# Attention stage: buffers of the first three weight blocks, engine of the last query rotation, and places of the value stores, a broadcast and five transpositions

## The chip, the core and the metric

The kernel runs on one core of a Trainium2 chip. The core has a matrix engine (TensorE, PE; its weight loads are shown apart as PEld), a vector engine (VectorE, DVE), a scalar engine (ScalarE, ACT), a general engine (GpSimd, POOL) and a queue engine (SyncE, SP) that only issues transfers. Each engine works through its own instructions in order; transfers (DMA) are issued by SP, ACT and POOL and run on 16 shared DMA engines. The metric is the device time of one launch in microseconds (us); less is better.

## The reference

One inference step of a two-layer encoder for 512 new tokens and 64 tokens of a running stream, 576 in all, 1024 features wide, in float32. Layer 0 mixes tokens by causal pooling; layer 1 is attention. Each is followed by an MLP with squared ReLU, and every sub-layer has an RMS normalisation ahead of it:

```python
for i in range(DEPTH):
    h = _rmsnorm(x, norm_mix[i])
    y = pool_mixer(h) if i == 0 else attn_mixer(h)
    x = x + y
    x = x + (relu(_rmsnorm(x, norm_mlp[i]) @ w_up[i]) ** 2) @ w_down[i]
```

The attention projects `h` by one matrix into 16 query heads of 64, 4 key and 4 value heads, 8 indexer queries of 64, one indexer key of 64 and 8 indexer weights. Queries, keys, indexer queries and indexer key are rotated: `x1*c - x2*s, x2*c + x1*s`, with halves x1, x2 of each head. The indexer scores `sum_h relu(qi_h . ki) * wi_h` select the best keys of each token (256, or fewer when there are few); softmax attention goes over the selected keys alone. New keys, values and indexer keys are outputs too.

## The kernel before

**Layout.** Activations lie with features on the 128 partitions and tokens along the free dimension, eight tiles of 128 x 576. Every float32 matrix product is done as three reduced-precision ones: each operand is split into an upper part (`act.copy`, line 206 for weights, 316 for activations) and a remainder (`dve.tensor_tensor`, lines 207 and 317), and upper x upper, remainder x upper and upper x remainder are summed in PSUM.

**Weights.** Weights come as blocks of 128 x 1024 (512 KB). One generator, `loaded`, holds the order of all blocks of the kernel (`jobs`, each with a kind), starts their loads some blocks ahead, and `next_block` hands out the split block; two more are kept split ahead (`AHEAD = 2`). A load needs a landing buffer from `raw_tile` (lines 139 to 145): in the stages of pooling and MLP the pool `raws` has two buffers, and a second pool `more` has two more, which are open only to loads called with `mlp=True`; these take turns, turns 0 and 1 of four to `raws`, 2 and 3 to `more`. Loads with `mlp=True` are issued by SP, the others by ACT. The split block itself takes one of three buffers of `weights`. In the attention stage the memory of `more` belongs to the pool `under`, which holds a pad, the rotation tables `cs` and `sn` and two masks.

**MLP of layer 0.** Its downward products go in pairs of output tiles by a scheme with seven products in place of eight. A pair (class `Pair`) has the products b11 and b21 in bank a, t1 and b22 in bank c, and t2, t3 and t4 in a seeded bank ("seed" in the rows). Between t3 and t4 VectorE must take t3 out of the bank into x (line 490); after opening, lines 486 do the same with a minus sign. The last pair's t4 ends the MLP.

**Attention.** `attention` (line 1087 on) first scales and splits x into `xs` (lines 316, 317), sends x to DRAM for later (`xd`, line 1093), and loads `cs` and `sn`. With TensorE's order written out by hand (`manual_schedule`) come the two indexer projections of the first four heads (`project_qi`, "pi" in the rows, 24 matmuls of 448 columns each), the token sums of the norm, the broadcast of the norm's factor over the partitions (two "rb" matmuls, evicted by ACT, line 357) and the indexer key ("ki"). POOL and VectorE multiply the factor into `cs` and `sn` (lines 1121, 1122). Then the indexer queries are rotated by VectorE (`rope` with `started`), the key is rotated, the eight indexer weights are transposed by five small "pw" matmuls (line 1197) into `wi` (line 1198), the other four indexer heads are projected, and the key and four query groups follow (`rope_q`, "pj"). For those ACT copies the two projections out of PSUM (lines 1150, 1151), POOL does four products, a difference and a sum with 576 columns (lines 1152 to 1158), ACT and POOL split the result (1161, 1162), and eight transfers of SP put it into DRAM as `qd` (line 1182). Index scores and the ranking of the keys (`top_k`, line 1258 on) run on VectorE beside this. Last comes the value projection ("v", line 1460), evicted by ACT to `V` (line 1462), and two stores of it by SP (lines 1463, 1464).

The scores, softmax, transpositions and value products follow as 40 units; two units share a `Group`, whose queries SP loads from `qd` (line 1349) into one of three slots with the tag "a". The groups go key head by key head for the first two blocks of 128 tokens, then block by block.

**What sets the order.** Except where `manual_schedule` fixes it, a planner orders the instructions of every engine and queue by a simulated timeline; `tc.issue_after` adds constraints to it.

Of the kernel before, what the change touches and what calls it, by code (L numbers as in the profile page):

```python
# [12 lines left out]
ALU = mybir.AluOpType  # L13
# [3 lines left out]
P = 128  # L17
D = 1024
KT = D // P
TP = 512  # L20
TS = 64
T = TP + TS
HT = T // 2
NKV = 4
NIDX = 8
# [26 lines left out]
def pool_dsa_kernel(ctx: ExitStack, tc: tile.TileContext, a, o):  # L52
    nc = tc.nc
    act, dve, pool, pe = nc.scalar, nc.vector, nc.gpsimd, nc.tensor
# [51 lines left out]
    def psum1(s="po", pool="po"):  # L106
        return phase[pool].tile([P, 512], F32, tag="po", name=uid(s))
# [12 lines left out]
    ident = const([P, P], "ident")  # L120
# [16 lines left out]
    last_of = {}  # L137
# [16 lines left out]
    jobs = []  # L154
# [32 lines left out]
                jobs.append(("made", "down", c, q) if layer else ("pair", *rows("down", layer, c, q)))  # L187

    mlp_jobs(0, 4, PLAIN[0])
    jobs.extend(("w_ki" if j == 0 else "w_in", a["w_in"][j]) for j in (1, 2, 0, *range(3, 15)))  # L190
    jobs.extend(("w_v", a["w_v"][j]) for j in range(2))
    for kind in ("w_o", "w_o2"):
        jobs.extend((kind, a["w_o"][m]) for m in range(KT))
# [53 lines left out]
    def loaded():  # L247

        waiting, held = [], 0
        while jobs or waiting:  # L250
            while jobs and held < (4 if "more" in phase else 2 if "third" in phase else 1) and ("last" in phase or jobs[0][0] not in ("pair", "made")):
                kind, *srcs = jobs.pop(0)
                if kind == "made":
                    r1, r2 = rows(srcs[0], 1, *srcs[1:])
                    m = mixed[:, pairs[tuple(srcs)]].rearrange("p a b -> p (a b)")
                    srcs = [r1, m[:, 1024:], m[:, :1024], r2[:, 512:]]
                mlp = kind in ("mlp", "pair", "made", "w_o2")
                waiting.append((kind, [load(src, src.shape[1], nc.sync if mlp else act, mlp)[:, :src.shape[1]] for src in srcs]))
                held += len(srcs)
            kind, tiles = waiting.pop(0)  # L260
            held -= len(tiles)
            yield kind, tiles
# [53 lines left out]
            act.activation(dst[:, 0], src, AF.Copy, scale=scale)  # L316
            dve.scalar_tensor_tensor(dst[:, 1], src, scale, f32(dst[:, 0]), ALU.mult, ALU.subtract)

    def project(pt, w, xs, between=iter(()), cols=((0, HT), (HT, HT)), ks=range(KT), ends=None):

        for k in ks:
            next(between, None)
            wh, wl = at(w, k)
            for i, (wt, part) in enumerate(((wh, 0), (wh, 1), (wl, 0))):
                for h, (c, m) in enumerate(cols):
                    pe.matmul(  # L326
                        pt[h][:, :m] if isinstance(pt, tuple) else pt[:, h, :m], wt, xs[k][:, part, c:c + m],
                        start=(k == (ends or ks)[0] and i == 0), stop=(k == (ends or ks)[-1] and i == 2),
                    )

    class Norm:
# [755 lines left out]
    def attention(parts):  # L1087
        nonlocal x
        norm = Norm("a")
        xs = split_x(2, norm, ["xs"] * KT)  # L1090
# [4 lines left out]
        cs, sn = (const([P, T], s, pool=phase["under"]) for s in ("cs", "sn"))  # L1095
        nc.sync.dma_start(cs, a["cos"])
        nc.sync.dma_start(sn, a["sin"])
        V = const([P, 9, 256], "V", pool=phase["cst1"])
        wi = const([P, 5, 8], "wi", pool=cst)
        nc.sync.dma_start(V[:, 4:8], a["cache_v"])  # L1100


        def project_qi(amid=None):
            pt = psum1("pi")
            w = next_block()
            for ks in (range(KT - 2), range(KT - 2, KT)) if amid else (range(KT),):
                if ks[0]:
                    amid()
                project((pt,), w, xs, cols=((P, T - P),), ks=ks, ends=(0, KT - 1))
            return pt[:, :T - P]  # L1110

        with tc.manual_schedule(engines={ENG.PE}):
            q0 = [project_qi()]
            norm.stats()
            r = norm.r
            two = psum("rb")
            q0.append(project_qi(lambda: norm.spread((two[:, 0], two[:, 1]))))
            rb = norm.rb
            pki = psum("ki")
            project(pki, next_block(), xs)  # L1120
        pool.tensor_tensor(cs, cs, rb, ALU.mult)
# [7 lines left out]
            split(t[:, :, :TP], raw[:, :TP], None, sub)  # L1129
            return t  # L1130

        def rope(started=None):

            pts = started
            if not started:
                pts = []
                for _ in range(2):
                    pt = psum("pj")
                    project(pt, next_block(), xs, between)
                    pts.append(pt[:, :, :HT])  # L1140
            n = T - P if started else T
            a1, b2, b1, a2 = (tmp("rp", "rp", 4)[:, :n] for _ in range(4))
            if started:
                pa, pb = pts
                dve.tensor_tensor(a1, pa, cs[:, P:], ALU.mult)
                dve.tensor_tensor(a2, pa, sn[:, P:], ALU.mult)
                dve.tensor_tensor(b2, pb, sn[:, P:], ALU.mult)
                dve.tensor_tensor(b1, pb, cs[:, P:], ALU.mult)
            else:
                act.copy(halves(a1), pts[0])  # L1150
                act.copy(halves(b1), pts[1])
                pool.tensor_tensor(a2, a1, sn, ALU.mult)
                pool.tensor_tensor(a1, a1, cs, ALU.mult)
                pool.tensor_tensor(b2, b1, sn, ALU.mult)
                pool.tensor_tensor(b1, b1, cs, ALU.mult)
            eng = dve if started else pool
            eng.tensor_tensor(a1, a1, b2, ALU.subtract)
            eng.tensor_tensor(b1, b1, a2, ALU.add)
            st = [pair_slot("b", "st")[:, :, :n] for _ in range(2)]
            for j, t in enumerate((a1, b1)):  # L1160
                act.copy(st[j][:, 0], t)
                pool.tensor_tensor(st[j][:, 1], t, f32(st[j][:, 0]), ALU.subtract)
            return (a1, b1), st
# [3 lines left out]
        def rope_qi(g, started):  # L1167

            _, st = rope(started)
            for h in range(4):  # L1170
                for j in range(2):
                    for part in range(2):
                        at = part * 64 + j * 32
                        nc.sync.dma_start(f32(qi[at:at + 32, 4 * g + h]), f32(st[j][32 * h:32 * h + 32, part]))

        def rope_q(s):

            _, st = rope()
            qd = dram.tile([4, 2, 2, 32, T], F32, tag=s, name=s)
            for h in range(4):  # L1180
                for j in range(2):
                    nc.sync.dma_start(qd[h, :, j].rearrange("a p t -> p a t"), f32(st[j][32 * h:32 * h + 32]))
            return qd.rearrange("h a j p t -> (a j p) h t")

        between = iter(())
# [3 lines left out]
        wt = tmp("wt")  # L1189
        act.copy(halves(wt[0:32]), pki[0:32, :, :HT])  # L1190
        for to, first, table in ((t1, 96, cs), (t2, 64, sn)):
            for i, c in enumerate((first, 160 - first)):
                dve.tensor_tensor(halves(to[32 * i:32 * i + 32]), pki[c:c + 32, :, :HT], halves(table[c:c + 32]), ALU.mult)
        pw = psum1("pw")
        for i in range(5):
            n = P if i < 4 else TS
            pe.transpose(pw[:n, 32 * i:32 * i + 32], wt[0:32, i * P:i * P + n], ident[0:32, 0:32])
            dve.tensor_scalar(wi[:n, i], pw[:n, 32 * i:32 * i + NIDX], r[:n, i:i + 1], NIDX ** -0.5, ALU.mult, ALU.mult)
        dve.tensor_tensor(ki[0:32], t1[0:32], t2[0:32], ALU.subtract)
        dve.tensor_tensor(ki[32:64], t1[32:64], t2[32:64], ALU.add)  # L1200
        nc.sync.dma_start(o["ki"], ki[0:64])
# [5 lines left out]

        cki = split_cache(a["cache_ki"], "cki", kis)

        rope_qi(1, [project_qi() for _ in range(2)])  # L1210

        work = [None] + [const([P, (i + 1) * P if i < 4 else TP + TS], f"work{i}", pool=phase[("cst1", "under", "under", "cst2")[i - 1]]) for i in range(1, 5)]

# [186 lines left out]
        def steps():  # L1400

            ranked = {0}
            for u in range(-4, total + 2):
                if 0 <= u + 4 < total and units[u + 4].s == 0:
                    v = units[u + 4]
                    groups[v.i, v.g] = Group(v.i, v.g)
                if 0 <= u < total:
                    units[u].transpose()
                if 0 <= u + 2 < total:
                    v = units[u + 2]  # L1410
                    if u + 2 >= 8:
                        next(index, None)
                    if v.i not in ranked:
                        ranked.add(v.i)
                        while done[0] < v.i * NIDX and next(index, 1) is None:
                            pass
                        top_k(v.i)
                    v.scores()
                if 0 <= u - 1 < total:
                    units[u - 1].values()  # L1420
                if 0 <= u - 2 < total and units[u - 2].s == 1:
                    units[u - 2].group.outputs()
                if u >= 18 and u % 2 == 0:
                    next(first_out, None)
                yield

        def pace():
# [20 lines left out]
                nc.sync.dma_start(f32(t[32 * c:32 * c + 32]), f32(st[c % 2][32 * g:32 * g + 32]))  # L1448
            ks.append(t)
        for g in range(NKV):  # L1450
            qd[g] = rope_q(f"q{g}")
        wv = [next_block(), next_block()]
        for i in range(5):
            n = P if i < 4 else TS
# [5 lines left out]
                    pe.matmul(pt[:n, :256], xs[k][:, part, i * P:i * P + n], wt,  # L1460
                              start=(k == 0 and j == 0), stop=(k == KT - 1 and j == 2))
            act.activation(V[:n, i if i < 4 else 8], pt[:n, :256], AF.Copy, scale=r[:n, i:i + 1])
        nc.sync.dma_start(o["v_p"], V[:, 0:4])
        nc.sync.dma_start(o["v_s"], V[:TS, 8])
        parts.close()
        parts.enter_context(stage(ps=3, po=2))
        for _ in steps():
# [125 lines left out]
```

## Time and profile before

| what | value |
|---|---|
| median of 3 runs | 1115.61 us (1115.17 to 1118.61) |
| profiled execution, its own time | 1115.93 us |
| its span in the profile | 1114.2 us |
| mean granted TensorE clock | 0.989 |
| TensorE busy | 97% of the span |
| VectorE, ScalarE, GpSimd busy | 71%, 50%, 26% |

The first layer's MLP ends near 441 us of the span; attention lasts until about 722 us; the second MLP fills the rest. A row of a timeline gives the start, the time until the group's end, engine, line, operation, output and inputs, shapes, count, and in brackets the idle time before it with the instruction that ended it. A row of the waits gives who waited for whom, microseconds in total, times and the longest. In a matrix engine's row the instructions overlap, so a row can be longer than the time until the next one starts.

### The profile page before, as it was taken

What the parts mean: (1) busy time and instruction counts of PE and PEld (TensorE: products, weight loads), DVE (VectorE), ACT (ScalarE), POOL (GpSimd) and SP (SyncE); (2) the same over time, 40 slices, a digit from 0 to 9 for tenths busy, and PEclk for the clock granted to TensorE, in tenths of its full rate; (3) what the DMA queues carried; (4) which work ended last, traced back from release to release, by engine and by line L of the source; (5) the groups of instructions that cost most, each with busy time, mean ns of one, the idle gap of its engine ahead of it and who ended that gap; (6) DMA issues with size and microseconds to landing.
All of it is one profiled execution on the core that took longest, in us unless ns stands there. A gap on an engine that the chain in (4) does not pass through costs nothing.

```text
span 1114.2 us, 20339 instructions
## 1 busy us (share of the span) xinstructions
PE 1082.3 (97%) x8027; PEld 1064.7 (96%) x8027; DVE 791.3 (71%) x1441; ACT 556.4 (50%) x939; POOL 295.2 (26%) x227
## 2 busy tenths in 40 slices
PE   8999999999999998999989999999999999999995
PEld 8999999999999988899979999999999999999995
DVE  7767656665755787679679993778758867865644
ACT  7544334334433454444378665755536636644542
POOL 2005514531451642157935342001000000000002
PEclk9999999999999998999989999999999999999998
DMA  7266489479668979357642432448575655455402
GB/s 238 62 166 160 134 225 273 118 201 268 158 171 232 243 205 251 106 154 190 188 150 58 126 97 93 141 124 218 163 235 176 197 166 165 157 161 171 143 19 85
DMA packets 81263, 183.54 MB, mean 165 GB/s; under 512 B 11809, under 2 KB 23376, under 8 KB 81168
## 3 DMA queue, kind: packets, MB, share of 16 engines
q1 hardware_dynamic: 64512, 143.94, 39.2%
q0 software_dynamic: 13056, 25.17, 13.7%
q10 hardware_dynamic: 3600, 13.14, 3.7%
q8 instruction: 63, 1.03, 0.4%
q14 instruction: 32, 0.26, 0.1%
HBM read 167.14 MB, written 61.22 MB: 205 GB/s over the span
## 4 chain that ended last, share of the span: by engine, by line
PE 73%; DVE 7%; DMA 7%; POOL 5%; issue 4%; ACT 3%; SPq 0%; DVEq 0%; POOLq 0%; ACTq 0%
PE seed L429 14%; PE up L587 13%; PE c L429 9%; PE a L429 9%; PE pj L326 6%; PE dn L326 4%; PE o L1334 3%; DVE w L207 2%; DMA raw<-in_w_down 2%; PE wa L326 2%; PE pi L326 2%; DMA mixed<-mixed 2%; PE sc L1295 1%; PE z L949 1%; PE pt L1315 1%
## 5 line engine op out<-in xcount | busy, mean ns | idle before, releaser
L206 ACT CAST w<-raw 128x1024 fp32r<-128x1024 f32 (+2 forms) x242 | 211.0, 889 | 215.8 <-PE seed L429 82.6
L207 DVE TENSOR_TENSOR w<-raw,w 128x1024 fp32r<-128x1024 f32 (+2 forms) x224 | 246.7, 1108 | 61.9 <-ACT w L206 61.3
L587 PE MATMUL up<-xs,w 128*128 128x288 f32 x1536 | 206.3, 295 | 0.0
L587 PEld LDWEIGHTS up<-xs,w 128*128 128x128 f32 x1536 | 204.0, 188 | 0.2
L429 PE MATMUL seed<-u,w 128*128 128x288 f32 x1008 | 147.9, 298 | 6.3 <-DVE x L490 3.3
L429 PEld LDWEIGHTS seed<-u,w 128*128 128x128 f32 x1008 | 139.4, 190 | 7.9 <-DVE x L490 3.5
L429 PE MATMUL c<-u,w 128*128 128x288 f32 x672 | 100.9, 297 | 2.0 <-DVE w L207 1.2
L429 PE MATMUL a<-u,w 128*128 128x288 f32 x672 | 100.0, 295 | 1.5 <-ACT w L206 1.2
L429 PEld LDWEIGHTS c<-u,w 128*128 128x128 f32 x672 | 93.2, 188 | 3.2 <-DVE w L207 1.7
L429 PEld LDWEIGHTS a<-u,w 128*128 128x128 f32 x672 | 93.0, 188 | 2.3 <-ACT w L206 1.7
L812 POOL TENSOR_TENSOR x<-x,spare 128x320 f32<-128x320 f32 (+1 forms) x9 | 8.2, 943 | 232.9 <-ACT spare L808 232.9
L326 PE MATMUL pj<-xs,w 128*128 128x288 f32 x480 | 67.7, 295 | 0.0
L236 POOL DMA_DIRECT2D mixed<-in_w_up x24 | 28.0, 1210 | 144.5 <-DMA mixed<-mixed 100.3
L326 PEld LDWEIGHTS pj<-xs,w 128*128 128x128 f32 x480 | 65.4, 188 | 0.9
L236 POOL DMA_DIRECT2D mixed<-in_w_down x24 | 27.6, 1274 | 139.7 <-DMA mixed<-mixed 88.9
L429 PE MATMUL seed<-bx,w 128*128 128x288 f32 x432 | 62.5, 296 | 0.0
L207 DVE TENSOR_TENSOR w<-sum,w 128x1024 fp32r<-128x1024 f32 (+1 forms) x32 | 34.6, 1080 | 37.0 <-ACT w L206 36.9
L285 POOL TENSOR_TENSOR sum<-raw 128x512 f32<-128x512 f32 x16 | 26.4, 1647 | 127.2 <-DMA raw<-in_w_down 119.4
L429 PEld LDWEIGHTS seed<-bx,w 128*128 128x128 f32 x432 | 59.3, 188 | 0.1
L206 ACT CAST w<-sum 128x1024 fp32r<-128x1024 f32 (+1 forms) x32 | 26.7, 834 | 59.8 <-POOL sum L290 52.9
L722 DVE SCALAR_TENSOR_TENSOR v<-up,rbm 128x288 f32<-128x288 f32 x80 | 32.6, 450 | 31.9 <-PE up L587 29.0
L587 PE MATMUL up<-bx,w 128*128 128x288 f32 x288 | 51.0, 295 | 0.7 <-DVE x L1481 0.7
(298 smaller groups left out, 2027.6 us busy)
## 6 DMA issues: line engine op xcount, KB each, us to landing
raw<-in_w_up SPq DMA_DIRECT2D x52, 512.0 KB, 5.0
raw<-in_w_down SPq DMA_DIRECT2D x52, 512.0 KB, 4.3
raw<-mixed SPq DMA_DIRECT2D x48, 512.0 KB, 4.2
mixed<-in_w_down POOLq DMA_DIRECT2D x24, 512.0 KB, 7.9
mixed<-mixed SPq DMA_DIRECT2D x24, 512.0 KB, 7.9
mixed<-in_w_up POOLq DMA_DIRECT2D x24, 512.0 KB, 9.5
raw<-in_w_in ACTq DMA_DIRECT2D x15, 512.0 KB, 4.0
mixed<-in_w_down SPq DMA_DIRECT2D x12, 512.0 KB, 6.3
```

The costliest lines, as they stand in the source:

```text
L206: act.copy(w[:, 0, at], src[:, at])
L207: how["sub"].tensor_tensor(w[:, 1, at], src[:, at], f32(w[:, 0, at]), ALU.subtract)
L236: pool.dma_start(to, add, accum_op=ALU.add)
L285: pool.tensor_tensor(s[:, :512], r2[:, :512], r2[:, 512:], ALU.add)
L326: pe.matmul(pt[h][:, :m] if isinstance(pt, tuple) else pt[:, h, :m], wt, xs[k][:, part, c:c + m], start=(k == (ends or ks)[0] and i == 0), ...
L429: pe.matmul(bank[:, :HT], wt[:, at], ut, start=first and j == 0 and i == 0, stop=j == 3 and i == 2, skip_group_check=True)
L587: pe.matmul(pt[h][:, :HT], w[:, wt, k * P:(k + 1) * P], moving(k, part, h), start=n == 0 and i == 0, stop=n == KT - 1 and i == 2)
L722: dve.scalar_tensor_tensor(v[:, 2 * i + h], pt[h][:, :HT], 0.0, halves(norm.rb)[:, h], ALU.max, ALU.mult)
L949: pe.matmul(z[s, i][:n, (g % 2) * 256:(g % 2 + 1) * 256], lhs, rhs, start=kk + j == 0, stop=kk == 1 and j == 2)
L1295: pe.matmul(pt[:, hh, :n], q[:, 2 * s + hh], ks[g][:, part, :n], start=part == 0, stop=part == 1)
L1315: pe.transpose(pp[:, c:c + P], pr[:, hh, kt * P:(kt + 1) * P], ident)
L1334: pe.matmul(oc[:, 2 * s + hh], pT[:, c:c + P], V[:, kt, vs], start=kt == 0, stop=kt == i)
```

## The change

1. The first three attention blocks (1, 2 and 0; two of indexer queries, which get the new kind `w_qi`, and the key's) are loaded like the MLP's: with `mlp=True`, so with turns over four buffers, and by SP.
2. The broadcast of the norm's factor is no longer put between the sixth and seventh eighth of the second projection but behind it; the arguments `amid` and `ends` go.
3. The last query group (`g == NKV - 1`) is rotated by VectorE straight out of PSUM, as the indexer queries are (`fast`): the two ACT copies and six POOL operations become six of VectorE; the split and the transfers stay.
4. The five transpositions of the indexer weights move behind the first of the two later indexer projections.
5. The two stores of the new values move from behind the value projection into the units, when their loop stands at unit 18, behind the query load issued last.

```diff
-    jobs.extend(("w_ki" if j == 0 else "w_in", a["w_in"][j]) for j in (1, 2, 0, *range(3, 15)))
+    jobs.extend(("w_ki" if j == 0 else "w_qi" if j < 3 else "w_in", a["w_in"][j]) for j in (1, 2, 0, *range(3, 15)))
...
-                mlp = kind in ("mlp", "pair", "made", "w_o2")
+                mlp = kind in ("mlp", "pair", "made", "w_o2", "w_qi", "w_ki")
...
-            q0.append(project_qi(lambda: norm.spread((two[:, 0], two[:, 1]))))
-            rb = norm.rb
+            q0.append(project_qi())
+            rb = norm.spread((two[:, 0], two[:, 1]))
             pki = psum("ki")
...
-        def rope(started=None):
+        def rope(started=None, fast=False):
...
+            fast = fast or bool(started)
...
-            if started:
+            if fast:
+                two = (lambda t: t) if started else halves
                 pa, pb = pts
-                dve.tensor_tensor(a1, pa, cs[:, P:], ALU.mult)
-                dve.tensor_tensor(a2, pa, sn[:, P:], ALU.mult)
-                dve.tensor_tensor(b2, pb, sn[:, P:], ALU.mult)
-                dve.tensor_tensor(b1, pb, cs[:, P:], ALU.mult)
+                for to, pt, table in ((a1, pa, cs), (a2, pa, sn), (b2, pb, sn), (b1, pb, cs)):
+                    dve.tensor_tensor(two(to), pt, two(table[:, T - n:]), ALU.mult)
...
-            eng = dve if started else pool
+            eng = dve if fast else pool
...
-        rope_qi(1, [project_qi() for _ in range(2)])
+        q1 = [project_qi()]
+        pw = psum1("pw")
+        for i in range(5):
...
+        q1.append(project_qi())
+        rope_qi(1, q1)
...
+                if u == 18:
+                    with tc.issue_after(last_of["sync"].ins):
+                        nc.sync.dma_start(o["v_p"], V[:, 0:4])
+                        nc.sync.dma_start(o["v_s"], V[:TS, 8])
...
-            qd[g] = rope_q(f"q{g}")
+            qd[g] = rope_q(f"q{g}", g == NKV - 1)
...
-        nc.sync.dma_start(o["v_p"], V[:, 0:4])
-        nc.sync.dma_start(o["v_s"], V[:TS, 8])
```

More of the change, by code (lines that the diff above doesn't have):

```diff
@@ L317, in split, with project @@
             dve.scalar_tensor_tensor(dst[:, 1], src, scale, f32(dst[:, 0]), ALU.mult, ALU.subtract)
-    def project(pt, w, xs, between=iter(()), cols=((0, HT), (HT, HT)), ks=range(KT), ends=None):
+    def project(pt, w, xs, between=iter(()), cols=((0, HT), (HT, HT)), ks=range(KT)):
         for k in ks:
@@ L327, in project @@
                         pt[h][:, :m] if isinstance(pt, tuple) else pt[:, h, :m], wt, xs[k][:, part, c:c + m],
-                        start=(k == (ends or ks)[0] and i == 0), stop=(k == (ends or ks)[-1] and i == 2),
+                        start=(k == ks[0] and i == 0), stop=(k == ks[-1] and i == 2),
                     )
@@ L1100, in attention, with project_qi @@
         nc.sync.dma_start(V[:, 4:8], a["cache_v"])
-        def project_qi(amid=None):
+        def project_qi():
             pt = psum1("pi")
             w = next_block()
[L1106 to L1109, printed above, removed]
+            project((pt,), w, xs, cols=((P, T - P),))
             return pt[:, :T - P]
@@ L1174, in rope_qi, with rope_q @@
                         nc.sync.dma_start(f32(qi[at:at + 32, 4 * g + h]), f32(st[j][32 * h:32 * h + 32, part]))
-        def rope_q(s):
-            _, st = rope()
+        def rope_q(s, fast):
+            _, st = rope(fast=fast)
             qd = dram.tile([4, 2, 2, 32, T], F32, tag=s, name=s)
@@ L1193, in attention @@
                 dve.tensor_tensor(halves(to[32 * i:32 * i + 32]), pki[c:c + 32, :, :HT], halves(table[c:c + 32]), ALU.mult)
[L1194 to L1198, printed above, removed]
         dve.tensor_tensor(ki[0:32], t1[0:32], t2[0:32], ALU.subtract)
@@ L1208, in attention @@
         cki = split_cache(a["cache_ki"], "cki", kis)
-        rope_qi(1, [project_qi() for _ in range(2)])
+        q1 = [project_qi()]
+        pw = psum1("pw")
+        for i in range(5):
+            n = P if i < 4 else TS
+            pe.transpose(pw[:n, 32 * i:32 * i + 32], wt[0:32, i * P:i * P + n], ident[0:32, 0:32])
+            dve.tensor_scalar(wi[:n, i], pw[:n, 32 * i:32 * i + NIDX], r[:n, i:i + 1], NIDX ** -0.5, ALU.mult, ALU.mult)
+        q1.append(project_qi())
+        rope_qi(1, q1)
         work = [None] + [const([P, (i + 1) * P if i < 4 else TP + TS], f"work{i}", pool=phase[("cst1", "under", "under", "cst2")[i - 1]]) for i in range(1, 5)]
```

## The prediction, made before the changed kernel was run

> **What bounds the kernel now.** I read the page's first parts, then what TensorE (PE) waited for, then the chain of waits and each engine's timeline around the two longest waits, last the stretches by granted clock.
>
> ```profile
> span 1114.2 us, 20339 instructions
> PE 1082.3 (97%) x8027; PEld 1064.7 (96%) x8027; DVE 791.3 (71%) x1441; ACT 556.4 (50%) x939; POOL 295.2 (26%) x227
> ...
> PE seed L429 <- DVE x L490: 3.3, 1, 3.3
> PE sc L1295 <- DMA q<-q: 2.9, 1, 2.9
> ...
> PE pw L1197 <- ACT wt L1190: 0.7, 1, 0.7
> ```
>
> PE is busy for 97% of the span, so nothing that runs beside it pays unless it ends a wait of PE. The two longest waits of PE, and the small one at pw, lie where the diff edits. The stretches around the two long ones (columns: length, then busy us of PE, PEld, DVE, ACT, POOL, then granted PE clock, DMA share, GB/s):
>
> ```profile
> 434.60:437.88 3.28, 0.00 (x1) 0.00 (x1) 1.11 (x3) 1.76 (x4) 0.00 (x0) 0.87 0.29 76
> 437.88:443.60 5.72, 5.72 (x20) 5.45 (x21) 4.18 (x7) 3.06 (x7) 0.35 (x2) 0.50 0.87 274
> 441.00:482.00 41.00, 39.79 (x230) 36.50 (x229) 28.14 (x54) 17.70 (x34) 7.62 (x6) 0.97 0.49 152
> 568.35:571.23 2.88, 0.01 (x2) 0.03 (x1) 0.70 (x3) 0.84 (x5) 0.00 (x0) 0.81 0.94 269
> 571.23:577.00 5.77, 5.77 (x28) 5.75 (x29) 3.65 (x15) 1.92 (x6) 0.00 (x0) 0.50 0.10 23
> 561.00:600.00 39.00, 34.05 (x255) 31.72 (x255) 34.30 (x142) 29.41 (x106) 21.22 (x17) 0.91 0.38 114
> ```
>
> After each long wait PE runs for 5.7 us at half clock. Each wait therefore costs more than its own length: half of 5.72 us, 2.86, comes on top at the first. The rows of "busy" hide this, for a slow matmul counts as busy. [...]
>
> **Part one, the first three blocks** (numbered 1, 2 and 0 in the weights, in order of use). Why PE idles at 434.6:
>
> ```profile
> 419.97 0.35 ACTq L149 DMA_DIRECT2D raw<-in_w_in  x1
> ...
> 430.14 5.90 DMA raw<-in_w_in
> 436.12 0.63 ACT w L206
> 436.77 0.69 DVE w L207
> 437.46 0.37 DVE x L490
> ```
>
> The last product of the MLP (t4) goes into the bank from which VectorE must first take t3 (L490, row x<-x,seed). VectorE works in order and has the split of the second block ahead of that, and the split waits for a load issued only at 430.14. It could not be issued earlier: both small "raws" buffers were taken. Now the places that the two other buffers ("more") offer:
>
> ```profile
> 417.17 1.38 DVE L207 TENSOR_TENSOR w<-raw,w 128x1024 fp32r<-128x1024 f32 x1
> ...
> 424.92 1.29 POOL L290 TENSOR_TENSOR sum<-sum,raw 128x512 f32<-128x512 f32 x1 [2.77 <-DVE w L207]
> ...
> 418.58 0.33 SPq L1096 DMA_DIRECT2D cs<-in_cos  x1
> 426.23 0.33 SPq L1097 DMA_DIRECT2D sn<-in_sin  x1
> 427.37 0.33 SPq L1093 DMA_DIRECT2D xd<-x  x1
> 441.65 0.33 SPq L1093 DMA_DIRECT2D xd<-x  x1
> ```
>
> The MLP makes 64 loads that count turns, so the three are turns 65 to 67: one in raws, two in "more". cs and sn lie in the memory of "more" (pad, cs, sn and two masks are 64+576+576+384+512 = 2112 floats, two buffers of 1056), and their loads start exactly when its buffers come free: 417.17+1.38 = 418.55, and 424.92+1.29 = 426.21. So the first block still goes out at 419.97, the second right behind it (about 420.3 instead of 430.14), the third at about 426.2.
>
> When do they land? The first block's load took 8.7 us in this crowded stretch:
>
> ```profile
> raw<-in_w_in ACTq DMA_DIRECT2D x1, 512.0 KB, 8.7
> ...
> cs<-in_cos SPq DMA_DIRECT2D x1, 288.0 KB, 9.1
> sn<-in_sin SPq DMA_DIRECT2D x1, 288.0 KB, 7.3
> ```
>
> Second block: 420.3 + 8.7 = 429, and up to 3 us more for standing behind the first on SP's queue, so 429 to 432. ACT then needs 1.1 us and VectorE another 0.7: done by 434, before t3 ends at 434.6. What is late next is t3's own way through VectorE, about 0.5 us (0.37 and two semaphores). The gap goes from 3.28 to 0.5, gain 2.78; a gap of 0.5 leaves the clock alone (the 0.7 us wait at pw does: the 0.97 of 441 to 482 is 1.2 us lost, no more than the half-clock time up to 443.6 that lies in it). **Together 2.78 + 2.86 = 5.64**, bounds 0 (the wait stays) and 6.1 (no gap at all).
>
> The cost side of the same edit: the three issues move from ACT's queue to SP's, 0.35 us each, beside stores that nobody waits for: 0. The copies for the second MLP's mixed weights, which SP may issue only behind its last load, now stand behind these three; nothing in this stage reads them: 0. cs now waits for the second block's split, sn for the third's. That split follows t4:
>
> ```profile
> 441.17 1.14 ACT L206 CAST w<-raw 128x512 fp32r<-128x512 f32 x2 [2.66 <-PE seed L429]
> ...
> 454.35 0.76 DVE L1122 TENSOR_TENSOR sn<-sn,rba 128x576 f32<-128x576 f32 x1 [3.36 <-ACT rba L357]
> ```
>
> It ends near 443.1 now, and near 438.7 when t4 starts 2.78 earlier and takes half as long (1.6 less). sn then lands 7.3 to 9.1 us later, 446 to 448; it is wanted at 454.35 - 5.6 + 1.3 (next part) = 450. Cover 2 us; beyond it VectorE stops, with rotations of the indexer's queries and block splits queued behind. Taken as 0.
>
> **Part two, broadcast and transpositions.** The two rb matmuls move behind six pi matmuls: no instruction more or fewer, the 0.5 us wait stays where they now stand, and cs, sn and what they feed come 6 x 7.03/33 = 1.3 us later. The transpositions of wt move behind a projection:
>
> ```profile
> 462.18 0.24 PE L1197 MATMUL pw<-ident,wt 32*128 32x32 f32 x1 [0.72 <-ACT wt L1190]
> 462.35 7.03 PE L326 MATMUL pi<-xs,w 128*128 128x448 f32 x33
> ...
> 481.83 0.48 DVE L1243 TENSOR_SCALAR work<-ix,wi 128x256 f32<-128x256 f32 x1
> ```
>
> PE's 0.72 us wait goes, since 24 matmuls of pi stand ahead and need nothing from wt. wi comes some 5 us later; its first reader in the index scores is at 481.83, 19 us after the first transposition. **Gain 0.72**, bounds -1 (an index score catches PE) and 0.72.
>
> **Part three, the last query group on VectorE, and the value stores.** Why PE idles at 568.35:
>
> ```profile
> 560.33 1.11 PE L1295 MATMUL sc<-k,q 128*128 128x128 f32 x8 [0.56 <-ACT V L1462]
> ...
> 558.02 3.65 SPq L1182 DMA_DIRECT2D q<-st  x8
> 561.76 0.77 SPq L1463 DMA_DIRECT2D out_v_p<-V  x1
> 562.63 1.10 SPq L1464 DMA_DIRECT2D out_v_s<-V  x1
> 563.85 7.24 DMA q<-q
> ...
> 572.46 0.42 DVE L1273 CUSTOM_DVE_ANT_0 p<-sc,work 128x256 f32<-128x256 f32 x1 [3.40 <-PE sc L1295]
> ...
> q<-q SPq DMA_DIRECT2D x1, 256.0 KB, 2.9
> ...
> raw<-in_w_o ACTq DMA_DIRECT2D x1, 512.0 KB, 4.4
> ```
>
> The fourth group's queries are issued at 563.85, behind q3's stores and both value stores, and take 7.24 us beside the values on their way out; the same load issued at 540 took 2.9. There are three q slots, so the load cannot start before the first group's scores end, near 561.1. With the stores gone it goes out then and lands at 564 to 566 (2.9, or 4.4 like the weight block issued at 560.9); PE wants it at 568.35. The wait of 2.88 ends. The half clock afterwards costs PE up to half of 5.77, but here VectorE may set the pace: in 561 to 600 it is busy 34.30 of 39, so no more than 4.70 can come out of that stretch, and in the next it is full. **I take 4.2**, bounds 0 and 4.7. I stand near the upper end because VectorE's idleness there is mostly this wait (3.40 us).
>
> The rotation: two ACT copies and six POOL operations go, six VectorE ones of some 0.76 us come (4.6 us; the 576-column product with sn above). Their second one writes a buffer that POOL frees at 547.4, the end of the row below. Behind it in VectorE's queue stand splits of the output weights, which PE reads tens of us later.
>
> ```profile
> 543.98 3.42 POOL L1162 TENSOR_TENSOR st<-rp,st 128x576 fp32r<-128x576 f32 x2 [0.98 <-ACT st L1161]
> ...
> 559.07 1.47 DVE L207 TENSOR_TENSOR w<-raw,w 128x512 fp32r<-128x512 f32 x2 [9.29 <-ACT w L206]
> ```
>
> VectorE idles 9.29 us there, which hides them; without that cover they would cost up to 4.6. By itself the faster rotation gains nothing: group 3 is wanted many units later; it only empties SP's queue earlier. The value stores reappear later, 1.9 us of SP time, between query loads that have several units' lead: 0.
>
> **Sum.** 5.64 + 0.72 + 4.2 = 10.6. Against the profiled execution's 1115.93 us (span 1114.2 and 1.7 around it) that is 1105.4. The median of the runs is 1115.61, 0.3 lower; so 1105.1.
>
> **The rivals.**
> *The second block lands late all the same.* On SP's queue it stands behind the first block and a residual store. If it lands at 436, nothing of part one is left: 1105.1 + 5.6 = 1110.7. For it: loads of this stretch take 7 to 9 us; against it: it starts ten microseconds earlier than now. [...]
>
> *The q wait is replaced.* VectorE or ACT (29.41 of 39 busy) takes the place of the load, or the load is late for another reason; part three gives 0 to 1: 1109 to 1109.5. For it: VectorE's 34.30 of 39; against: it idled through the wait.
>
> *The change doesn't do what it says*, both long waits stay and only pw goes: 1114.9.
>
> *Slower: SP's queue holds the blocks back.* SP issues in order, and four residual stores in the same stretch wait for finished x, the fourth until 441.65. If the planner puts the three loads behind that one, the first block is there at 442 + 8.7 = 450.7 instead of about 441, PE idles some 10 us more, and with parts two and three gained the time is 1115.6 + 10 - 4.9 = 1121. It decides at whether the first load leaves before 427 or after 441. Against it: cs and sn, written behind all four stores in the program, leave before the third (426.23, 427.37), so the planner orders by readiness.
>
> **How the numbers follow.** Chances: forecast 0.62 (its own range 1103 to 1108), late block 0.13, replaced q wait 0.13, both waits stay 0.06, slower 0.06. Some 0.3% (1112.3 to 1119) is what a measurement tells from no change: faster 0.62 + 0.13 + 0.13 less 0.02 for a late block that ends above 1112.3, 0.86; within 0.08; slower 0.06. The range reaches from 1102 (all upper bounds, 11.5, and 2 for orders that the planner improves) to 1111.5, which takes in either wait staying but not both.
>
> **What would show it.** Right: no row "PE seed <- DVE x L490" over 1 us; no row "PE sc <- DMA q<-q"; granted clock 1.00 in the stretches after both places; no wait at pw; the second block's load issued on SP near 420. Wrong: a half-clock stretch of 5 us in either place, a wait of VectorE for sn, or more PE idle time in 575 to 640 with "DVE" or "ACT" as its releaser.

## The result and the profile after

The changed kernel takes 1105.11 us (median of 3 runs) against 1115.62 us of the kernel before on the same chip: a ratio of 0.9905, 95% interval 0.988 to 0.9931. Two disturbed executions, 1496.63 us here and 2117.58 us with the blocks alone below, are left out of all medians and ratios. Run again on another chip it took 1105.41 us (6 runs) against 1116.79, ratio 0.9896 (0.9867 to 0.9926). The forecast was 1105.1.

The changed kernel's profiled execution took 1107.12 us. Its page and its waits of TensorE (PE) between 430 and 660 us of the span, who waited for whom, us in total, times, longest:

```profile
span 1105.3 us, 20345 instructions
PE 1078.4 (98%) x8027; PEld 1060.7 (96%) x8027; DVE 795.5 (72%) x1447; ACT 554.5 (50%) x937; POOL 283.7 (26%) x221
```

```profile
PE v L1463 <- DVE w L207: 0.9, 1, 0.9
PE seed L429 <- DVE x L490: 0.8, 1, 0.8
PE sc L1294 <- ACT V L1465: 0.6, 1, 0.6
```

The waits of 3.3 us (t4), 2.9 us (query load) and 0.7 us (transpositions) are gone; t4 keeps 0.8. The row at v is new: TensorE waits for a split of the value weights. To see what each part is worth I cut both executions at the same instructions: first matmul of t3, first value matmul (v), first score, first score against the cached keys. The stretches of the kernel before, in that order (length, busy us of PE, PEld, VectorE, ACT, POOL, granted clock, DMA share, GB/s):

```profile
432.83:545.50 112.67, 108.19 (x717) 103.74 (x716) 89.29 (x185) 47.89 (x92) 56.91 (x38) 0.97 0.57 166
545.50:560.30 14.80, 14.28 (x122) 14.01 (x120) 4.06 (x4) 6.63 (x14) 13.89 (x10) 1.00 0.61 171
560.30:660.60 100.30, 95.32 (x755) 91.35 (x755) 93.74 (x309) 72.53 (x208) 41.00 (x35) 0.97 0.36 108
```

And of the changed kernel:

```profile
433.80:539.30 105.50, 104.71 (x717) 100.99 (x716) 86.15 (x174) 45.51 (x89) 54.62 (x39) 1.00 0.62 175
539.30:555.60 16.30, 14.89 (x122) 14.23 (x120) 11.54 (x22) 5.99 (x13) 6.24 (x4) 1.00 0.70 197
555.60:650.40 94.80, 92.60 (x753) 88.57 (x754) 92.30 (x309) 72.45 (x208) 40.92 (x35) 1.00 0.37 108
```

The first stretch is 7.17 us shorter, the third 5.50 (5.4 by the exact starts, as in the table), the second 1.50 longer: 11.2 us won between t3 and the cached keys. The span fell by only 8.9. This execution reached t3 0.97 us later, before anything that was changed: its clock stood at half for 6.8 us in the first 45 us of the span, and for 3.4 in the profile of before. Another 1.1 us went behind the last downward product of the second MLP: there TensorE waited 1.20 us for VectorE in place of 0.49, and its last broadcast, now at half clock, took 1.19 in place of 0.67. Whole executions scatter by several us (the kernel before from 1111.25 to 1118.83 in 17 runs on one chip), so below the verdicts rest on these stretches, and the whole times stand beside them.

| kernel | t3 to v | v to first score | first score to cached keys | whole, median us | ratio to before (95%) |
|---|---|---|---|---|---|
| before | 112.7 | 14.8 | 100.2 | 1115.6 to 1116.8 | |
| changed, first profile | 105.5 | 16.3 | 94.8 | 1105.11 | 0.9905 (0.988 to 0.9931) |
| changed, run again | 105.5 | 14.8 | 94.9 | 1105.41 | 0.9896 (0.9867 to 0.9926) |
| blocks alone | 107.6 | 14.8 | 98.8 | 1110.89 | 0.995 (0.9932 to 0.9969) |
| late value stores alone | 112.1 | 14.8 | 95.1 | 1111.03 | 0.9966 (0.9946 to 0.9986) |
| VectorE rotation alone | 108.7 | 14.8 | 95.8 | 1111.06 | 0.9955 (0.9939 to 0.9971) |
| changed, rotation undone | 105.6 | 14.9 | 94.9 | 1105.81 | 0.9907 (0.988 to 0.9933) |
| changed, value stores early | 105.6 | 16.2 | 96.6 | 1106.45 | 0.9914 (0.9886 to 0.9943) |
| changed, transpositions early | 108.1 | 14.9 | 94.8 | 1105.24 | 0.9902 (0.9887 to 0.9917) |
| changed, broadcast early | 106.1 | 15.3 | 94.8 | 1104.95 | 0.9898 (0.9882 to 0.9914) |
| changed, blocks on ACT's queue | 105.6 | 14.8 | 94.9 | 1104.56 | 0.9892 (0.9875 to 0.991) |
| changed, two output blocks on SP | 105.6 | 16.2 | 94.9 | 1104.91 | 0.99 (0.9877 to 0.9922) |
| changed, value split on POOL | 105.6 | 14.8 | 94.8 | 1103.32 | 0.9882 (0.9858 to 0.9906) |
| changed, both of these | 105.6 | 14.9 | 94.8 | 1104.31 | 0.9897 (0.9873 to 0.9921) |

### The profile page after: what moved, and what is told of

The parts are those of the page before. It is cut to its first block, busy times and chain, and to the rows that moved or that the text cites. A ratio compares the mean times of both kernels' runs of the same rounds, so it can differ in the third digit from the quotient of the medians.

```text
span 1105.3 us, 20345 instructions
## 1 busy us (share of the span) xinstructions
PE 1078.4 (98%) x8027; PEld 1060.7 (96%) x8027; DVE 795.5 (72%) x1447; ACT 554.5 (50%) x937; POOL 283.7 (26%) x221
## 3 DMA queue, kind: packets, MB, share of 16 engines
q8 instruction: 63, 1.03, 0.4%
## 4 chain that ended last, share of the span: by engine, by line
PE 58%; DVE 12%; issue 3%; POOL 3%; DMA 3%; ACT 2%; DVEq 0%; SPq 0%; ACTq 0%; POOLq 0%
PE seed L429 13%; PE c L429 8%; PE a L429 8%; PE up L587 7%; PE dn L326 4%; DVE w L207 3%; PE o L1333 2%; PE wa L326 2%; PE pi L326 2%; PE pj L326 2%; DVE work L1258 1%; DMA raw<-in_w_down 1%; PE pt L1314 1%; PE sc L1294 1%; DMA mixed<-in_w_up 1%
## 5 line engine op out<-in xcount | busy, mean ns | idle before, releaser
L285 POOL TENSOR_TENSOR sum<-raw 128x512 f32<-128x512 f32 x16 | 23.8, 1487 | 129.1 <-DMA raw<-in_w_down 129.1
L326 PE MATMUL dn<-u,w 128*128 128x288 f32 (+2 forms) x384 | 51.7, 295 | 0.0
```

What stands on the lines that cost most here:

```text
L285: pool.tensor_tensor(s[:, :512], r2[:, :512], r2[:, 512:], ALU.add)
L326: pe.matmul(pt[h][:, :m] if isinstance(pt, tuple) else pt[:, h, :m], wt, xs[k][:, part, c:c + m], start=(k == ks[0] and i == 0), stop=(k = ...
```

## The experiments

**The changed kernel again**

No edit; a second profile says what of the first was chance.

> The changed kernel again, as the yardstick of the runs beside it. Its first runs gave 1104.9 to 1107.1 us, so 1105 to 1107; the profile should again show TensorE waiting once for the split of the value weights (PE v <- DVE w, 0.9 us) and no long wait at the end of the MLP or at the first units.

Measured: 1105.41 us, the same lengths in the first and third stretch, no wait at v. That wait belongs to some executions only.

**The blocks alone**

```diff
# the kernel before, and only:
-    ... "w_ki" if j == 0 else "w_in", a["w_in"][j]) for j in (1, 2, 0, ...
+    ... "w_ki" if j == 0 else "w_qi" if j < 3 else "w_in", a["w_in"][j]) for j in (1, 2, 0, ...
-    mlp = kind in ("mlp", "pair", "made", "w_o2")
+    mlp = kind in ("mlp", "pair", "made", "w_o2", "w_qi", "w_ki")
```

> The kernel before with only the loads of the first three blocks changed (buffers and queue). My theory: the gap of 3.3 us before the MLP's last product shrinks to 0.8 and the 5.7 us at half clock behind it go too, together 5.1 to 5.4 us: about 1110.3; granted clock 1.00 from 435 to 450 us. Rival: the half clock costs little because other things pace that stretch, and only the shorter wait counts, 2.5 us: 1113.1.

Measured: t3 to v 107.6, so part one is worth 5.1 us: the wait of t4 went from 3.28 to 0.8 (2.5), and PE's busy time from 108.19 to 105.58 (2.6, the half clock). The stretch in this run:

```profile
431.08:538.67 107.59, 105.58 (x718) 101.22 (x716) 89.23 (x185) 46.80 (x90) 58.04 (x39) 1.00 0.60 173
```

The wait for the query load stayed, 2.58 us.

**The blocks in the same buffers, on ACT's queue**

```diff
-    load(src, src.shape[1], nc.sync if mlp else act, mlp)
+    load(src, src.shape[1], nc.sync if mlp and kind not in ("w_qi", "w_ki") else act, mlp)
```

> The changed kernel with its first three blocks in the MLP's buffers as now, but their loads issued on ACT's queue as before. If the buffers alone end the wait for the second block (the prediction's step): t3 to t4 stays 2.6 us and t3 to v 105.5; 1105 for the whole. If the queue does it, because an issue on ACT stands behind ACT's own work and its wait for a free buffer: the second block lands late again, t3 to t4 above 3 us with a row 'PE seed <- DVE x', and up to 5.6 of the gain is gone (1110.7), or ACT's work of the MLP behind the waiting issue is late and shows as waits before t3.

Measured: t3 to t4 2.56 us, t3 to v 105.55, 1104.56 us. The loads leave at 418.3, 418.7 and 424.6 on ACT's queue and serve as well as on SP's. The four buffers earn the gain; the other queue earns nothing. From issue to landing the block loads issued between 415 and 430 us took 8.2 us on ACT's queue here (median of four) and 8.1 on SP's in the changed kernel (median of three).

**The transpositions early again**

```diff
-        q1 = [project_qi()]
         pw = psum1("pw")   # and the five transpositions, now ahead of ki's subtraction
-        q1.append(project_qi())
-        rope_qi(1, q1)
+        rope_qi(1, [project_qi() for _ in range(2)])
```

> The changed kernel with the transpositions of wt put back to their old place, ahead of the key's subtraction; the broadcast stays late. Counted from the first t3 matmul to the first v matmul (112.7 us before, 107.6 with the first three blocks alone, 105.5 in the changed kernel, so part two is worth 2.1). If the transpositions earn only their wait of 0.7 (the prediction's step): a row 'PE pw <- ACT wt' of about 0.7 is back and the stretch is 106.2. If the order of the projections that they allow earns the rest as well: 107.6. If they earn nothing because pw then stands behind a projection anyway: 105.5.

Measured: t3 to v 108.1, beyond every number expected. The transpositions' late place is worth 2.6 us, and a second wait says why. TensorE's timeline in this run:

```profile
446.84 0.65 PE L356 MATMUL rb<-diag,ones 128*128 128x288 f32 x2
448.52 0.75 PE L356 MATMUL rb<-diag,ones 128*128 128x288 f32 x2 [1.04 <-ACT rba L357]
...
456.37 0.24 PE L1194 MATMUL pw<-ident,wt 32*128 32x32 f32 x1 [0.72 <-ACT wt L1187]
```

The same instructions in the changed kernel:

```profile
451.07 0.65 PE L356 MATMUL rb<-diag,ones 128*128 128x288 f32 x2
451.34 3.21 PE L326 MATMUL pi<-xs,w 128*128 128x448 f32 x14
454.38 0.65 PE L356 MATMUL rb<-diag,ones 128*128 128x288 f32 x2
...
465.14 0.24 PE L1206 MATMUL pw<-ident,wt 32*128 32x32 f32 x1
```

With the transpositions behind the next projection, the planner could pull that projection forward: 10 of its matmuls stand ahead of the first broadcast and 14 between the two, whose second waits for ACT to evict something. So two waits end, 0.72 and 1.04. The other 0.84 us lie in TensorE's busy time (105.59 in this run, 104.75 in the changed kernel), some 0.5 of it around the broadcasts.

**The broadcast early again**

```diff
-            q0.append(project_qi())
-            rb = norm.spread((two[:, 0], two[:, 1]))
+            q0.append(project_qi(lambda: norm.spread((two[:, 0], two[:, 1]))))
+            rb = norm.rb
```

> The changed kernel with the broadcast put back amid the first projection; the transpositions stay late. From the first t3 matmul to the first v matmul, 105.5 us in the changed kernel. If the broadcast's place earns nothing, as the prediction has it: 105.5, with a wait of at most 0.5 at rb. If the 1.4 us of part two that the prediction does not explain come from the broadcast: 106.9, and a row with rb or with what reads it among PE's waits.

Measured: 106.05, between the two. The late broadcast earns 0.5 us where the transpositions are late. Where they are early it costs 0.5 (108.1 against 107.6 with the blocks alone). Part two's two moves belong together: 2.1 us in all.

**The late value stores alone**

```diff
# the kernel before, and only: the two stores of V leave their place behind the value projection
+                if u == 18:
+                    with tc.issue_after(last_of["sync"].ins):
+                        nc.sync.dma_start(o["v_p"], V[:, 0:4])
+                        nc.sync.dma_start(o["v_s"], V[:TS, 8])
```

> The kernel before with nothing but the value stores late (blocks, broadcast, transpositions and rotation as before). From the first v matmul to the first score against the cached keys: 115.1 us before. If the value stores alone hold the query load (the prediction's step): no row 'PE sc <- DMA q<-q', the stretch is 109.7 to 110.9 (4.2 to 5.4 less), and the whole about 1111, some 4.5 below the kernel before. If the fourth group's own stores (3.65 us of SP time from 558.0, to 561.7) hold it too, the load leaves at 561.7 and lands at 564.6 to 569: a wait of up to 0.7 and a stretch of 111 to 112. If the late rotation on VectorE is needed as well: a wait of 2 us or more, and 114.

Measured: no wait for the query load; v to the cached keys 109.9 us in place of 115.1. The load leaves at 561.22 instead of 563.85, and it is faster too. Issues in a short window, KB each and us from issue to landing, first the kernel before, then this run:

```profile
out_v_p<-V SPq DMA_DIRECT2D x1, 512.0 KB, 5.5
q<-q SPq DMA_DIRECT2D x1, 256.0 KB, 7.2
```

```profile
q<-q SPq DMA_DIRECT2D x1, 256.0 KB, 5.3
```

**The rotation by VectorE alone**

```diff
# the kernel before, and only:
-            qd[g] = rope_q(f"q{g}")
+            qd[g] = rope_q(f"q{g}", g == NKV - 1)   # with rope(fast=...) as in the change
```

> The kernel before with nothing but the fourth query group rotated by VectorE (blocks, broadcast, transpositions as before; value stores in their old place). From the first v matmul to the first score against the cached keys: 115.1 us before. If the faster rotation alone earns nothing (the prediction's words): a row 'PE sc <- DMA q<-q' of 2.5 us or more, and 114 to 115. If it empties SP's queue early enough that the query load leaves as soon as its slot is free, some 2 us earlier than in the kernel before, and the load then only suffers from the value stores' traffic (7.1 us beside them, 4.4 to 5.5 without them): a wait of 0.5 to 1 us on the load, no half clock, and 111.0 to 112.5; the whole about 1112.5.

Measured: no wait for the query load at all, v to the cached keys 110.6, 4.5 us less than before. The fourth group's stores are out of SP's queue 11.8 us after the first value matmul (at 554.2) instead of 16.2, so the value stores go at 554.41 and 557.20 and the query load at 558.37, as its slot comes free; it took 3.6 us. (The wait for the second block was 1.9 us in this execution, where the kernel before had 3.3, and the clock did not fall: that, and not the edit, makes t3 to v 108.7.)

**Rotation undone, and value stores early, in the changed kernel**

```diff
# first run:
-            qd[g] = rope_q(f"q{g}", g == NKV - 1)
+            qd[g] = rope_q(f"q{g}", False)
# second run: the two stores of V back behind the value projection
```

> The changed kernel with the last query group rotated by GpSimd again. My theory: the rotation on VectorE is what delays the split of the value weights; without it that wait of 0.9 us in the rows (1.4 us of TensorE's time between the end of the query projections and the first scores) goes, and the fourth group's queries still land in time, since the value stores are out of SP's queue: 1.4 us less than the changed kernel, about 1104. Rival: the faster rotation is needed to empty SP's queue; its eight stores then end near the moment when the slot comes free, the query load takes up to 7 us, TensorE waits again for q by 0.7 to 3 us, and the kernel is 0 to 4 us slower than the changed one: 1106 to 1110.

> The changed kernel with the two value stores back in their old place. My theory: they again stand between the end of the value projection and the fourth group's query load, which then leaves about 2 us later and takes 5 to 7 us beside the 512 KB of values: TensorE waits 1 to 2 us for q, too short for the half clock, so 1 to 2 us slower than the changed kernel: about 1107.5. Rival A: the faster rotation alone ended the wait and the stores do no harm: no difference. Rival B: the old wait of 2.9 us comes back with its half clock: 4 to 5 us slower, about 1111.

Measured: without the rotation nothing changes locally (v to the cached keys 109.8). With the value stores early the query load leaves at 556.23, in time, but beside their 512 KB it takes 7.1 us where the changed kernel's takes 4.4:

```profile
out_v_p<-V SPq DMA_DIRECT2D x1, 512.0 KB, 6.0
...
q<-q SPq DMA_DIRECT2D x1, 256.0 KB, 7.1
```

It lands near 563.3, and TensorE, which wants it at 562.9, stops. The profile puts the wait down to an ACT cast that ended at 563.5; in the changed kernel the same scores start 0.4 us ahead of that cast, so they don't need it. TensorE's row, then that of VectorE, which waits behind:

```profile
563.51 0.71 PE L1294 MATMUL sc<-k,q 128*128 128x256 f32 x4 [0.58 <-ACT ot L1376]
```

```profile
564.26 0.42 DVE L1272 CUSTOM_DVE_ANT_0 p<-sc,work 128x256 f32<-128x256 f32 x1 [0.62 <-PE sc L1294]
```

That the load is what TensorE waits for is inferred from the times; the row does not name it. The third stretch is 1.7 us longer than in the other changed kernels, and only the first 0.6 to 0.8 of it are located here. (The rotation alone, which has the same early stores, is 0.7 us longer there than the late stores alone; that is not located either.)

**The new wait at v**

Where the wait of 0.9 us shows, the second value block's split ends 3.6 us after the first value matmul; where it doesn't, 2.2 us (the changed kernel run again), and 0.8 us ahead of it in the kernel before. Between them the cost is gradual: with the broadcast early the split ends 2.7 us after, and v to the first score is 15.3 us. TensorE and VectorE in the changed kernel's first profile:

```profile
539.34 2.77 PE L1463 MATMUL v<-w,xs 128*128 128x256 f32 x20
542.99 2.29 PE L1463 MATMUL v<-w,xs 128*128 128x256 f32 x17 [0.88 <-DVE w L207]
```

```profile
540.34 0.75 DVE L207 TENSOR_TENSOR w<-raw,w 128x528 fp32r<-128x528 f32 x1
542.20 0.73 DVE L207 TENSOR_TENSOR w<-raw,w 128x528 fp32r<-128x528 f32 x1
```

Ahead of it on ACT stands a load that waits for a buffer (7.1 to 7.7 us), and on VectorE the ranking of the keys. Two edits tell them apart:

```diff
# first run: the first two loads of the output weights on SP
-    load(src, src.shape[1], nc.sync if mlp else act, mlp)
+    load(src, src.shape[1], nc.sync if mlp or kind == "w_os" else act, mlp)   # "w_os": w_o, m < 2
# second run: the second value block's remainder taken by POOL
-            how["sub"].tensor_tensor(w[:, 1, at], ...)
+            (sub or how["sub"]).tensor_tensor(w[:, 1, at], ...)   # sub=pool for that block
# third run: both
```

> The changed kernel with the first two loads of the output weights issued on SP's queue instead of ACT's, nothing else. In the changed kernel ACT stands 7.1 to 7.7 us at such an issue before it casts the second value block, whose split ended 2.2 to 3.6 us after the first v matmul (0.8 before it in the kernel before), and where it was 3.6 late PE waited at v for 0.9. If ACT's held cast makes that split late: the split ends 1 us or less after the first v matmul, and v to the first score is 14.8. If VectorE's own queue of work sets it (it is busy 31.1 of 32.1 us ahead): the cast comes some 6 us earlier and the split still ends 2 to 3.6 us after the first v matmul. The whole 1105 by both.

> The changed kernel with the second value block's split done by POOL instead of VectorE (two operations), nothing else. If VectorE's queue sets the end of that split: it ends about 541, 1.7 us after the first v matmul where the changed kernel had 2.2 to 3.6, no row 'PE v <- ... w', v to the first score 14.8 us, and with it 1.5 us less than the profiled execution of the changed kernel, 0 less than its second one: 1104 to 1105.5 for the whole. If ACT's held cast sets it, the end stays at 2.2 to 3.6 and the wait at v can come back. A third way: POOL's stores of the third query group are 2.5 us later, and a query load or PE's scores wait for them: a new row with q among PE's waits.

> The changed kernel with both of the last two edits: the first two loads of the output weights on SP's queue, and the second value block's split on POOL. If each removes one of two things that the split stands behind: it ends before the first v matmul, with no wait at v and 14.8 us to the first score; the stretch from the first v matmul to the first score against the cached keys stays 109.7. If VectorE, freed of two splits of 0.75, sets the pace of that stretch: up to 1.5 less, 108.2. If SP's queue holds the third group's stores behind the loads: above 110. The whole 1103.5 to 1105.5.

Measured: with ACT freed, the cast comes at 531.61 instead of 537.25, and the split still ends at 541.2, 3.5 us after the first value matmul (537.7), with a wait of 0.8. ACT's row and VectorE's last half of this run:

```profile
531.61 1.17 ACT L206 CAST w<-raw 128x528 fp32r<-128x528 f32 x2 [3.73 <-PE pj L326]
```

```profile
540.47 0.70 DVE L207 TENSOR_TENSOR w<-raw,w 128x528 fp32r<-128x528 f32 x1
```

So VectorE's own queue sets it. With the split on POOL it ends at 537.4, 0.1 us ahead of the first value matmul, and the wait is gone:

```profile
534.75 2.61 POOL L207 TENSOR_TENSOR w<-raw,w 128x528 fp32r<-128x528 f32 x2
```

No query load is late from it. With both edits the split ends at 536.7, again 0.1 ahead, and v to the cached keys stays 109.7: VectorE, freed of 1.5 us, does not make that stretch shorter. The loads on SP's queue earn nothing, alone or beside the split on POOL. The kernel with that split alone had the lowest median, 1103.32 us, though its interval (0.9858 to 0.9906) and the changed kernel's overlap; what is shown is the stretch, 1.4 to 1.5 us shorter than in the executions that wait and no shorter than in the one that does not.

## Why the prediction was right, and where its steps were off

The sum, 10.6, came out: 10.5 and 11.4 us by the medians of the two sets of runs. By the stretches it is 5.1 + 2.1 + 5.4 = 12.6, or 11.1 where the new wait costs its 1.5. Each of the three terms was off, and the errors went in different directions; that the first median, 1105.11, meets the forecast of 1105.1 is partly luck. Two slips in the working change nothing: by its own row the query slot comes free at 561.4 (560.33 + 1.11), not near 561.1, and a part three of 0 to 1 would give that rival 1108.3 to 1109.3, not 1109 to 1109.5.

**Part one, 5.64 predicted, 5.1 measured.** Right in mechanism: the second block was held by its buffer. The three loads left where the prediction put them, and cs and sn later; SP's timeline in the changed kernel:

```profile
420.80 0.81 SPq L149 DMA_DIRECT2D raw<-in_w_in  x2
...
427.14 0.34 SPq L149 DMA_DIRECT2D raw<-in_w_in  x1
...
439.16 0.43 SPq L1096 DMA_DIRECT2D cs<-in_cos  x1
440.23 0.33 SPq L1097 DMA_DIRECT2D sn<-in_sin  x1
```

The gap left was 0.8, not 0.5, which is 0.3 of the difference; the half clock gave back 2.61, not 2.86. Both are sizes of one execution: with the old loads the wait was 3.28 us in the kernel before, 3.74 with the late value stores alone and 1.92 with the rotation alone. sn was wanted at 450 by the prediction, with a cover of 2 us; it was read at 456.4, because a whole projection now stood ahead of the second broadcast, and landed 5.4 us after its issue, at 445.6. The rival that a full SP queue keeps the blocks back fell by these rows, and the late block by the 0.8.

**Part two, 0.72 predicted, 2.1 measured.** The step that failed is "the 0.5 us wait stays where they now stand", and with it the costing of the two moves one by one. By itself the late broadcast makes that wait 1.04; with the transpositions out of the way the planner fills it with a projection. What was priced as one wait removed was the freedom to put a projection between the two broadcasts.

**Part three, 4.2 predicted, 5.4 measured, less 1.5 in some executions.** The wait and its half clock ended. The bound of 4.70, all of VectorE's idleness from 561 to 600, was no bound: the same work (239 of PE's rows, 132 of VectorE's) in the kernel before, then in the changed one:

```profile
561.03:597.55 36.52, 31.79 (x239) 29.72 (x239) 31.85 (x132) 27.58 (x100) 19.77 (x16) 0.91 0.40 121
```

```profile
556.33:587.45 31.12, 29.18 (x239) 27.04 (x239) 30.82 (x132) 27.49 (x100) 19.75 (x17) 1.00 0.38 107
```

It is 5.40 shorter: VectorE idles 0.30 where it idled 4.67, and its busy time is 1.03 less. Of that, 0.63 is one operation at the end of the ranking (`TENSOR_SCALAR work<-work`, 128 x 384), which took 1.29 us before and 0.66 after; why, and where the rest lies, stays open. VectorE does set the pace afterwards, as the step had it.

"By itself the faster rotation gains nothing" failed. Alone it ends the wait as well as the late value stores do (110.6 and 109.9 against 115.1), because emptying SP's queue earlier was itself the remedy; the prediction named that effect and gave it no value. Beside late value stores it earns nothing (109.8 without, 109.7 with). The edits were alternatives.

The rival "the q wait is replaced" was half true: the replacement came 20 us earlier than I looked, at v, once part two had moved TensorE 2 us closer to VectorE's queue. With the blocks alone the split ended 0.8 us ahead of v, with the transpositions early 0.5 behind it. "Splits of the output weights behind it" was the step: the split that mattered belonged to the value weights and stood between the rotation's instructions. Undoing the rotation leaves it 2.3 us behind v, so in the changed kernel the rotation is not shown to be its cause. But the rotation does take margin: with the rotation alone the split ends 0.5 us behind v, where the kernel before had it 0.8 ahead; the rotation's first product then stands between the split's two halves, and the second half takes 1.30 us. VectorE in the kernel before, then with the rotation alone:

```profile
543.39 1.32 DVE L207 TENSOR_TENSOR w<-raw,w 128x528 fp32r<-128x528 f32 x2
```

```profile
540.28 0.70 DVE L207 TENSOR_TENSOR w<-raw,w 128x528 fp32r<-128x528 f32 x1
540.90 0.75 DVE L1148 TENSOR_TENSOR rp<-pj,cs 128x576 f32<-128x576 f32 x1
541.56 1.30 DVE L207 TENSOR_TENSOR w<-raw,w 128x528 fp32r<-128x528 f32 x1
```

## What to carry to other kernels

When two edits shorten the same queue ahead of one late transfer, price them as alternatives, not as terms; and when an edit takes an instruction out of a hand-written or planned order, look for the waits that its neighbours can now fill, for here they made the edit worth three times the wait that it removed. After a gain on the bounding engine, list what other engines have to deliver next and by how little they were early: two us won at one place and a rotation put on VectorE each took from the value split's margin.

## What the runs showed of the clock

I had taken the half clock as what a long wait brings and a short one doesn't (2.88 us against 0.7). In the traces the length alone does not tell. In the kernel before, the granted clock fell at 437.03 and 570.15 and rose at 24.02, 443.86 and 576.98; the distances are whole multiples of 3.41 us (133.12 is 39 of them), and so they are in five other traces: both of the changed kernel, the blocks alone, the late value stores alone and the rotation alone. Cut into such stretches, counted from these changes, the kernel before (busy PE is the second number, the clock the third from the end):

```profile
433.62:437.03 3.41, 0.98 (x8) 0.74 (x6) 0.45 (x2) 0.91 (x2) 0.00 (x0) 1.00 0.31 122
437.03:440.44 3.41, 2.56 (x10) 2.56 (x11) 2.79 (x5) 1.48 (x3) 0.35 (x2) 0.50 0.76 193
440.44:443.86 3.42, 3.42 (x11) 3.15 (x11) 2.50 (x5) 2.60 (x5) 0.00 (x0) 0.50 0.96 337
...
566.74:570.15 3.41, 1.61 (x15) 1.37 (x14) 2.28 (x12) 2.40 (x11) 0.00 (x0) 1.00 0.93 299
570.15:573.57 3.42, 2.34 (x11) 2.37 (x12) 1.11 (x5) 0.58 (x3) 0.00 (x0) 0.50 0.27 70
```

With the blocks alone, at the query load:

```profile
558.94:562.35 3.41, 2.44 (x20) 2.07 (x19) 3.24 (x17) 3.37 (x15) 0.00 (x0) 1.00 0.95 319
562.35:565.76 3.41, 1.67 (x15) 1.70 (x16) 0.92 (x5) 0.40 (x2) 0.00 (x0) 1.00 0.55 150
565.76:569.17 3.41, 3.41 (x18) 3.36 (x18) 3.38 (x12) 2.47 (x10) 0.00 (x0) 0.50 0.30 79
```

With the rotation alone, at waits of 2.1 and 1.7 us in the MLP and at the 1.9 us before t4:

```profile
388.39:391.80 3.41, 1.26 (x9) 1.02 (x8) 3.39 (x7) 2.87 (x6) 0.00 (x0) 1.00 1.09 252
391.80:395.21 3.41, 3.41 (x17) 3.41 (x16) 2.41 (x6) 0.80 (x2) 0.00 (x0) 0.50 0.92 288
...
419.11:422.52 3.41, 1.83 (x14) 1.86 (x14) 3.41 (x6) 2.51 (x3) 2.26 (x2) 1.00 0.97 137
422.52:425.93 3.41, 3.41 (x27) 3.36 (x26) 3.39 (x6) 0.06 (x1) 0.23 (x1) 1.00 1.06 303
...
436.18:439.59 3.41, 2.21 (x15) 2.18 (x16) 3.32 (x6) 2.14 (x5) 0.35 (x2) 1.00 0.73 178
439.59:443.00 3.41, 3.41 (x19) 3.12 (x18) 2.97 (x6) 2.29 (x5) 0.00 (x0) 1.00 0.94 319
```

In these rows stretches in which PE was busy for 0.98, 1.26, 1.61 and 1.67 of 3.41 us were followed by one at half clock; those with 1.83, 2.21 and 2.44 were not. The same cut through the six traces, from 30 to 1080 us of each span, gives five stretches with 1.67 or less, each followed by half clock, and none with 1.83 or more that was. At both ends of the span the count fails: the changed kernel kept its clock after a stretch with 1.65 (from 6.33 us, first profile), all six lost it between 18.9 and 20.7 us, after stretches with 2.67 to 3.41, and beyond 1080 us two lost it after about 2.5 (the blocks alone, the late value stores alone). The 2.67 is the kernel before:

```profile
17.19:20.60 3.41, 2.67 (x23) 2.44 (x23) 3.41 (x13) 2.64 (x9) 0.31 (x1) 1.00 0.99 378
20.60:24.02 3.42, 3.32 (x15) 3.32 (x16) 3.28 (x18) 2.88 (x7) 0.00 (x0) 0.50 0.66 220
```

Most rows of that stretch are token sums, products of two columns; whether that has to do with the clock is not shown.

In the rows above, stretches at half clock with 2.56 and 2.34 busy were followed by another at half, those with 3.32 to 3.42 by the full clock. So what these waits cost beyond their length came in steps of 3.41 us at half clock, 1.7 us each where PE was busy throughout (half of 3.41): none for the 1.9 us wait, of which 0.72 us lay in one stretch and 1.20 in the next, one for the 2.58, two for the 3.28 and the 2.88, which were still going on when the clock fell. Those two steps cost half of what PE was busy in them, about 3.0 and 2.9 us. With the late value stores alone a wait of 3.74 us had one. So the wait before t4, with the old loads, brought two steps, one and none in three executions. Such differences fit part of the scatter of whole times: over the 51 runs of the kernel before that stood beside the experiments, time and mean granted clock go together with a correlation of -0.70, about half of the variance.
